# A batched matrix product: loads of four batches at a time, 32 partitions each, with the transposes on VectorE

## The chip, the cores and the metric

The kernel runs on one core of one Trainium2 chip. The metric is the device time of one execution in microseconds; lower is better. The time given for a kernel is the median over several executions. A profile is one execution, recorded by the hardware profiler; its own span is a little shorter than the device time, which also holds what lies around the span.

## The reference

For each of 32 batches, a 256 x 512 matrix is multiplied by a 512 x 384 matrix, all in float32 in memory:

```python
batch, dim_i, dim_j, dim_k = 32, 256, 512, 384
x: (batch, dim_i, dim_j) float32;  y: (batch, dim_j, dim_k) float32
return np.einsum('bij,bjk->bik', x, y).astype(np.float32)
```

TensorE contracts over the partitions of its two operands. y has the contracted index j as its rows already. x has i as its rows, so x has to be transposed on the chip before it can be the stationary operand. Both kernels multiply in float16 and accumulate in float32.

## The kernel before, in words

One batch is one step. In `load(b)` the x of a batch goes to a tile of 128 partitions, partition p holding rows 2p and 2p+1 (L59, runs of 4 KB), and y to a tile whose partition q holds rows 4q to 4q+3 (L60, runs of 6 KB). Both tiles have seven buffers, and loads are issued `AHEAD = 5` batches early. All DMAs, loads and stores, are issued by SyncE (SP) in one queue.

`transpose(b)` takes, for each of the four remainders t of j modulo 4, the columns t, t+4, t+8, ... of x, and transposes two blocks of 128 x 128 on TensorE against an identity matrix (L68), so that partition q of the result holds column 4q+t, in line with y. The result lies in PSUM; VectorE (L70) and ScalarE (L72) copy it to SBUF in turn, rounding to float16 on the way. `round_y(b)` rounds the four slices of y to float16, two on ScalarE (L79) and two on VectorE (L81). `multiply(b)` does 8 matmuls (L92) of 128 contraction rows, 128 output rows and 384 columns into two PSUM tiles. `collect(b)` copies them to SBUF, one on ScalarE (L107), one on VectorE (L109), and `store(b)` writes the batch out (L120, runs of 3 KB).

The order on each engine is the order in which the program is written: every operation is wrapped in `keep`, which holds it in program order. The main loop is a software pipeline: step s issues the loads of batch s+5, collects batch s-2, transposes and rounds batch s, multiplies batch s-1, and stores batch s-2. So the transposes of one batch stand between the multiplications of its neighbours. PSUM is divided into four buffers for transposes and four for results.

Of the kernel before, what the change touches and what calls it, by code (L numbers as in the profile page):

```python
# [1 line left out]

# [5 lines left out]


MM_DT = mybir.dt.float16  # L10
F32 = mybir.dt.float32
P = 128
AHEAD = 5
GROUPS = [1, 1, 1, 1, 1, 1, 1, 1, 1, 1, 1, 1, 1, 1, 1, 1, 1, 1, 1, 1, 1, 1, 1, 1, 1, 1, 1, 1, 1, 1, 1, 1]

@with_exitstack
def kernel(
    ctx: ExitStack,  # L20
    tc: tile.TileContext,
    x: bass.AP,
    y: bass.AP,
    out: bass.AP,
):
    nc = tc.nc

    B, I, J = x.shape
    _, _, K = y.shape

    NI = I // P
    NJ = J // P

    const_pool = ctx.enter_context(tc.tile_pool(name="const", bufs=1))
    x_pool = ctx.enter_context(tc.tile_pool(name="x_pool", bufs=AHEAD + 2))
    y_pool = ctx.enter_context(tc.tile_pool(name="y_pool", bufs=AHEAD + 2))
    yr_pool = ctx.enter_context(tc.tile_pool(name="yr_pool", bufs=4))
    xt_pool = ctx.enter_context(tc.tile_pool(name="xt_pool", bufs=4))
    o_pool = ctx.enter_context(tc.tile_pool(name="o_pool", bufs=8))
    tpsum_pool = ctx.enter_context(tc.tile_pool(name="tpsum", bufs=4, space=bass.MemoryType.PSUM))  # L40
    opsum_pool = ctx.enter_context(tc.tile_pool(name="opsum", bufs=4, space=bass.MemoryType.PSUM))


    keep = tc.keep_in_program_order

    identity = const_pool.tile([P, P], F32)
    make_identity(nc, identity)


    place = [(g, i, n) for g, n in enumerate(GROUPS) for i in range(n)]  # L50
    assert len(place) == B
    x_of, y_of, yr_of, xt_of, ps_of, o_of = {}, {}, {}, {}, {}, {}

    def load(b):


        x_of[b] = x_pool.tile([P, NI, J], F32, name="x_sb")
        y_of[b] = y_pool.tile([P, NJ, K], F32, name="y_sb")
        keep(nc.sync.dma_start(out=x_of[b], in_=x[b].rearrange("(p r) j -> p r j", p=P)))  # L59
        keep(nc.sync.dma_start(out=y_of[b], in_=y[b].rearrange("(q t) k -> q t k", q=P)))  # L60

    def transpose(b):
        x_sb = x_of.pop(b)
        xt_of[b] = xt_pool.tile([P, NJ, NI, P], MM_DT, name="xt_sb")
        for t in range(NJ):
            t_ps = tpsum_pool.tile([P, NI, P], F32, name="t_ps")
            for r in range(NI):
                keep(nc.tensor.transpose(t_ps[:, r], x_sb[:, r, t::NJ], identity))  # L68
            if t % 2 == 0:
                keep(nc.vector.tensor_copy(xt_of[b][:, t], t_ps))  # L70
            else:
                keep(nc.scalar.copy(xt_of[b][:, t], t_ps))  # L72

    def round_y(b):
        y_sb = y_of.pop(b)
        yr_of[b] = yr_pool.tile([P, NJ, K], MM_DT, name="y_r")
        for t in range(NJ):
            if t % 2 == 0:
                keep(nc.scalar.copy(yr_of[b][:, t], y_sb[:, t]))  # L79
            else:  # L80
                keep(nc.vector.tensor_copy(yr_of[b][:, t], y_sb[:, t]))  # L81

    def multiply(b):
        xt_sb, y_r = xt_of.pop(b), yr_of.pop(b)
        ps_of[b] = [
            opsum_pool.tile([P, K], F32, name=f"o_ps_{r}", tag="o_ps")
            for r in range(NI)
        ]
        for t in range(NJ):
            for r in range(NI):  # L90
                keep(
                    nc.tensor.matmul(  # L92
                        ps_of[b][r],
                        xt_sb[:, t, r],
                        y_r[:, t],
                        start=(t == 0),
                        stop=(t == NJ - 1),
                    )
                )

    def collect(b):
        g, i, n = place[b]
        if i == 0:
            o_of[g] = o_pool.tile([P, n, NI, K], F32, name="o_sb", tag=f"o_sb_{min(n, 2)}")
        for r in range(NI):
            if r % 2 == 0:
                keep(nc.scalar.copy(o_of[g][:, i, r], ps_of[b][r]))  # L107
            else:
                keep(nc.vector.tensor_copy(o_of[g][:, i, r], ps_of[b][r]))  # L109
        del ps_of[b]  # L110

    def store(b):
        g, i, n = place[b]
        if i < n - 1:
            return
        o_sb = o_of.pop(g)
        dst = out[b - i : b + 1].rearrange("b (p r) k -> p b (r k)", p=P)
        src = o_sb.rearrange("p b r k -> p b (r k)")
        if n == 1:
            keep(nc.sync.dma_start(out=dst[:, 0], in_=src[:, 0]))  # L120

    for b in range(AHEAD):
        load(b)
    for s in range(B + 2):
        if s + AHEAD < B:
            load(s + AHEAD)
        if s >= 2:
            collect(s - 2)
        if s == B - 1:
            multiply(s - 1)  # L130
        if s < B:
            transpose(s)
            round_y(s)
        if 1 <= s != B - 1 and s <= B:
            multiply(s - 1)
        if s >= 2:
            store(s - 2)


# [1 line left out]
_INS = ['x', 'y']  # L141
_OUTS = [((32, 256, 384), 'float32')]


# [23 lines left out]
```

## Time and profile before

| what | us |
|---|---|
| median of 7 runs | 137.52 (137.13 to 137.62) |
| the profiled execution | 137.17 |
| its span | 135.4 |
| PE busy in the span | 82.3 |
| VectorE (DVE) busy | 64.5 |
| ScalarE (ACT) busy | 66.7 |
| a load of x, issue to landing (median) | 10.2 |
| a load of y, issue to landing (median) | 11.2 |
| a store, issue to landing (median) | 10.9 |

PE is the matmul part of TensorE and PEld its weight loads, which overlap PE. Lines such as L92 are those of the kernel before. Busy time counts work of an engine alone, without the time in which it waits. From memory 41.94 MB are read, and 12.58 MB are written.

### The profile page before, as it was taken

What the parts mean: (1) busy time and instruction counts of PE and PEld (TensorE: products, weight loads), DVE (VectorE), ACT (ScalarE), POOL (GpSimd) and SP (SyncE); (2) the same over time, 40 slices, a digit from 0 to 9 for tenths busy, and PEclk for the clock granted to TensorE, in tenths of its full rate; (3) what the DMA queues carried; (4) which work ended last, traced back from release to release, by engine and by line L of the source; (5) the groups of instructions that cost most, each with busy time, mean ns of one, the idle gap of its engine ahead of it and who ended that gap; (6) DMA issues with size and microseconds to landing.
All of it is one profiled execution on the core that took longest, in us unless ns stands there. A gap on an engine that the chain in (4) does not pass through costs nothing.

```text
span 135.4 us, 1739 instructions
## 1 busy us (share of the span) xinstructions
PE 82.3 (61%) x512; PEld 57.4 (42%) x512; DVE 64.5 (48%) x160; ACT 66.7 (49%) x161; POOL 0.7 (1%) x6
## 2 busy tenths in 40 slices
PE   0589788857255775555775555775555775559610
PEld 0466555525333554333554333554333554435400
DVE  0445766656146644546644546644546644546510
ACT  3357666666056644446644446644446644446610
POOL 2000000000000000000000000000000000000000
PEclk9999999999999999999999999999999999999996
DMA  4999999999999999999999999999999999999992
GB/s 166 418 416 420 418 414 414 375 420 422 409 422 414 426 418 421 416 417 418 428 417 420 416 421 420 426 420 418 414 422 424 413 417 424 418 417 418 412 418 113
DMA packets 13833, 54.64 MB, mean 404 GB/s; under 512 B 1536, under 2 KB 1536, under 8 KB 13824
## 3 DMA queue, kind: packets, MB, share of 16 engines
q1 hardware_dynamic: 13824, 54.53, 98.8%
q8 instruction: 4, 0.07, 0.2%
q14 instruction: 5, 0.04, 0.1%
HBM read 41.94 MB, written 12.58 MB: 403 GB/s over the span
## 4 chain that ended last, share of the span: by engine, by line
DMA 80%; PE 10%; DVE 2%; SPq 2%; issue 1%; ACT 0%; ACTq 0%
DMA x_sb<-in_x_dram 31%; DMA y_sb<-in_y_dram 25%; DMA out_dram<-o_sb 24%; PE o_ps L92 6%; PE t_ps L68 4%; DVE o_sb L109 2%; SPq L59 1%; SPq L60 1%; ACT y_r L79 0%; SPq L120 0%; ACTq L79 0%
## 5 line engine op out<-in xcount | busy, mean ns | idle before, releaser
L68 PE MATMUL t_ps<-identity,x_sb 128*128 128x128 f32 x256 | 39.9, 301 | 45.8 <-DMA x_sb<-in_x_dram 43.2
L68 PEld LDWEIGHTS t_ps<-identity,x_sb 128*128 128x128 f32 x256 | 34.4, 211 | 56.7 <-DVE o_sb L109 42.1
L72 ACT CAST xt_sb<-t_ps 128x256 f16<-128x256 f32 x64 | 23.8, 373 | 54.5 <-issue 43.1
L70 DVE CAST xt_sb<-t_ps 128x256 f16<-128x256 f32 x64 | 27.1, 424 | 48.2 <-PE t_ps L68 46.3
L92 PE MATMUL o_ps<-y_r,xt_sb 128*128 128x384 f16 x256 | 47.4, 329 | 1.2 <-ACT y_r L79 1.2
L79 ACT CAST y_r<-y_sb 128x384 f16<-128x384 f32 x64 | 29.6, 509 | 6.4 <-DMA y_sb<-in_y_dram 6.3
L92 PEld LDWEIGHTS <-xt_sb 128*128 128x128 f16 x256 | 25.7, 100 | 14.8 <-issue 1.9
L81 DVE CAST y_r<-y_sb 128x384 f16<-128x384 f32 x64 | 20.1, 356 | 12.5 <-DMA y_sb<-in_y_dram 12.2
L109 DVE COPY o_sb<-o_ps 128x384 f32<-128x384 f32 x32 | 17.8, 557 | 4.6 <-PE o_ps L92 3.1
L107 ACT COPY o_sb<-o_ps 128x384 f32<-128x384 f32 x32 | 15.1, 472 | 1.2 <-PE o_ps L92 1.2
L72 ACT ACT_TABLE_LOAD x1 | 1.3, 1283 | 0.7 <-PEq L152 0.7
masks.py:199 POOL TENSOR_SCALAR_AFFINE_SELECT identity<-identity 128x128 f32<-128x128 f32 x1 | 0.3, 293 | 0.1
masks.py:197 POOL MEMSET identity<- 128x128 f32 x1 | 0.2, 206 | 0.3 <-POOLq L152 0.3
L152 POOL MEMSET const-bfloat16-1.0<- 128x1 bf16 x1 | 0.1, 102 | 0.0
L152 POOL MEMSET const-uint8-127<- 128x1 uint8 x1 | 0.1, 102 | 0.0
L152 POOL MEMSET const-float32-0.0<- 128x1 f32 x1 | 0.1, 99 | 0.2 <-issue 0.2
L152 POOL MEMSET const-float32-1.0<- 128x1 f32 x1 | 0.1, 99 | 0.0
## 6 DMA issues: line engine op xcount, KB each, us to landing
y_sb<-in_y_dram SPq DMA_DIRECT2D x32, 768.0 KB, 11.2
x_sb<-in_x_dram SPq DMA_DIRECT2D x32, 512.0 KB, 10.2
out_dram<-o_sb SPq DMA_DIRECT2D x32, 384.0 KB, 10.9
```

The lines of the kernel that those rows point to most:

```text
L59: keep(nc.sync.dma_start(out=x_of[b], in_=x[b].rearrange("(p r) j -> p r j", p=P)))
L60: keep(nc.sync.dma_start(out=y_of[b], in_=y[b].rearrange("(q t) k -> q t k", q=P)))
L68: keep(nc.tensor.transpose(t_ps[:, r], x_sb[:, r, t::NJ], identity))
L70: keep(nc.vector.tensor_copy(xt_of[b][:, t], t_ps))
L72: keep(nc.scalar.copy(xt_of[b][:, t], t_ps))
L79: keep(nc.scalar.copy(yr_of[b][:, t], y_sb[:, t]))
L81: keep(nc.vector.tensor_copy(yr_of[b][:, t], y_sb[:, t]))
L92: nc.tensor.matmul(ps_of[b][r], xt_sb[:, t, r], y_r[:, t], start=(t == 0), stop=(t == NJ - 1),)
L107: keep(nc.scalar.copy(o_of[g][:, i, r], ps_of[b][r]))
L109: keep(nc.vector.tensor_copy(o_of[g][:, i, r], ps_of[b][r]))
L152: nc = _bacc.Bacc("TRN2", target_bir_lowering=False, num_devices=1)
```

## The change

Four batches (a "quad") are one step now, and there are eight steps. x of a quad is loaded by one DMA: batch g of the four lies on partitions 32g to 32g+31, each partition holding 8 whole rows of x, one run of 16 KB. y likewise: partition q of a batch's 32 holds rows 16q to 16q+15 of y, one run of 24 KB. In the last quad the load of y is cut in two.

The identity and the TensorE transposes are gone. ScalarE rounds x to float16 and reorders it in the same copy (four copies of 1024 elements per partition, read in steps of 16 float32 elements). VectorE then transposes blocks of 32 x 32 (`nc.vector.transpose`, eight instructions of 512 elements per quad), each group of 32 partitions within itself. After that, partition q of a batch holds the columns 16q+c of x, for c from 0 to 15, in line with y.

Each matmul contracts over 32 partitions only, so a quad has 128 matmuls of 32 x 128 x 384 where four batches had 32 of 128 x 128 x 384. The innermost loop runs over the four batches, so consecutive matmuls use different groups of 32 partitions and different PSUM tiles. The eight PSUM tiles of a quad are all that there are.

y is rounded in eight chunks of 768 elements, five on VectorE and three on ScalarE. In the main loop a quad is transposed, rounded, multiplied and collected to the end before the next is begun; its stores are issued one step later (`LATE = 8`). x and y each have two buffers of a quad: the loads issued in step n are y of quad n+1 and x of quad n+2.

```diff
+Q = 4
+LATE = 8
+LAST = 2
+ROUND = (1, 0, 1, 1, 0, 1, 0, 1)
...
+    S = P // Q
+    R = I // S
+    C = J // S
+    NE = I // P
+    H = R // NE
+    N = B // Q
+    x_pool = ctx.enter_context(tc.tile_pool(name="x_pool", bufs=2))
+    xr_pool = ctx.enter_context(tc.tile_pool(name="xr_pool", bufs=1))
+    xt_pool = ctx.enter_context(tc.tile_pool(name="xt_pool", bufs=2))
+    y_pool = ctx.enter_context(tc.tile_pool(name="y_pool", bufs=2))
+    yr_pool = ctx.enter_context(tc.tile_pool(name="yr_pool", bufs=2))
+    o_pool = ctx.enter_context(tc.tile_pool(name="o_pool", bufs=12))
+    psum_pool = ctx.enter_context(tc.tile_pool(name="psum", bufs=Q * NE, space=bass.MemoryType.PSUM))
...
+    def load_x(n):
+        x_of[n] = x_pool.tile([P, R, J], F32, name="x_sb")
+        keep(nc.sync.dma_start(out=x_of[n],
+                in_=x[n * Q : (n + 1) * Q].rearrange("g (p r) j -> (g p) r j", r=R)))
+    def load_y(n):
+        y_of[n] = y_pool.tile([P, C, K], F32, name="y_sb")
+        src = y[n * Q : (n + 1) * Q].rearrange("g (p c) k -> (g p) c k", c=C)
+        w = C // (LAST if n == N - 1 else 1)
+        for c in range(0, C, w):
+            keep(nc.sync.dma_start(out=y_of[n][:, c : c + w], in_=src[:, c : c + w]))
+    def transpose_x(n):
+        x_sb = x_of.pop(n)
+        xr = xr_pool.tile([P, R, C, S], MM_DT, name="x_r")
+        xt_of[n] = xt_pool.tile([P, C, NE, S, H], MM_DT, name="xt_sb")
+        for h in range(H):
+            rows = slice(h * NE, (h + 1) * NE)
+            keep(nc.scalar.copy(xr[:, rows], x_sb[:, rows].rearrange("q r (j c) -> q r c j", c=C)))
+            for e in range(NE):
+                keep(nc.vector.transpose(xt_of[n][:, :, e, :, h], xr[:, h * NE + e]))
+    def round_y(n):
+        y_sb = y_of.pop(n)
+        y_r = yr_pool.tile([P, C, K], MM_DT, name="y_r")
+        w = C // len(ROUND)
+        for k, dve in enumerate(ROUND):
+            part = slice(k * w, (k + 1) * w)
+            if dve:
+                keep(nc.vector.tensor_copy(y_r[:, part], y_sb[:, part]))
+            else:
+                keep(nc.scalar.copy(y_r[:, part], y_sb[:, part]))
+        return y_r
...
+    def multiply(n, y_r):
+        xt_sb = xt_of.pop(n)
+        ps = [[psum_pool.tile([P, K], F32, name="o_ps") for e in range(NE)] for g in range(Q)]
+        for c in range(C):
+            for e in range(NE):
+                for g in range(Q):
+                    rows = slice(g * S, (g + 1) * S)
+                    keep(nc.tensor.matmul(ps[g][e],
+                            xt_sb[rows, c, e].rearrange("q p h -> q (p h)"),
+                            y_r[rows, c], start=(c == 0), stop=(c == C - 1)))
+        return ps
...
+    def collect(n, ps):
+        for g in range(Q):
+            o_sb = o_of[n * Q + g] = o_pool.tile([P, NE, K], F32, name="o_sb")
+            for e in range(NE):
+                if e % 2 == 0:
+                    keep(nc.scalar.copy(o_sb[:, e], ps[g][e]))
+                else:
+                    keep(nc.vector.tensor_copy(o_sb[:, e], ps[g][e]))
     def store(b):
+        keep(nc.sync.dma_start(out=out[b].rearrange("(m e) k -> m e k", m=P), in_=o_of.pop(b)))
+    load_x(0)
+    load_y(0)
+    load_x(1)
+    for n in range(N + 1):
+        if n + 1 < N:
+            load_y(n + 1)
+        if n + 2 < N:
+            load_x(n + 2)
+        if n < N:
+            transpose_x(n)
+            collect(n, multiply(n, round_y(n)))
+        for b in range(max((n + 1) * Q - LATE, 0), min((n + 2) * Q - LATE, B) if n < N else B):
+            store(b)
```

The lines of the kernel before that these replace are the functions printed above.

## The prediction

> **What bounds the kernel now.** I read the page from the top: the slices (is a resource full throughout?), the chain, the costliest groups (prices), then the trace in windows and as a timeline (what one step looks like).
>
> ```profile
> span 135.4 us, 1739 instructions
> ...
> DMA  4999999999999999999999999999999999999992
> ...
> DMA packets 13833, 54.64 MB, mean 404 GB/s; under 512 B 1536, under 2 KB 1536, under 8 KB 13824
> ...
> DMA 80%; PE 10%; DVE 2%; SPq 2%; issue 1%; ACT 0%; ACTq 0%
> ```
> The 16 DMA engines are full from the first slice to the last, and 80% of the chain that ended last is transfers. Now windows (us, then busy of PE, PEld, DVE, ACT, POOL, then clock, DMA share, GB/s):
>
> ```profile
> 60.00:80.00 20.00, 12.52 (x80) 8.72 (x80) 10.18 (x25) 10.23 (x25) 0.00 (x0) 1.00 1.02 420
> ...
> 131.00:132.00 1.00, 0.00 (x0) 0.00 (x0) 0.00 (x0) 0.00 (x0) 0.00 (x0) 1.00 1.05 421
> 132.00:133.00 1.00, 0.00 (x0) 0.00 (x0) 0.00 (x0) 0.00 (x0) 0.00 (x0) 1.00 0.61 243
> ```
> 420 GB/s in the steady part, still full at 132, while DVE and ACT are half idle. A batch is 1.70 MB (0.52 + 0.79 + 0.39), so 4.06 us at 420, 16.2 us for four; 54.5 MB is 130 us. The rest of the span is start and end. So only fewer bytes, a higher rate or a shorter end would gain; and the engines may slow down until four batches take 16.2 us. Their prices, in groups by line (busy, mean ns, idle and its releaser):
>
> ```profile
> L70 DVE CAST xt_sb<-t_ps 128x256 f16<-128x256 f32 x64 | 27.1, 424 | 48.2 <-PE t_ps L68 46.3
> L92 PE MATMUL o_ps<-y_r,xt_sb 128*128 128x384 f16 x256 | 47.4, 329 | 1.2 <-ACT y_r L79 1.2
> L79 ACT CAST y_r<-y_sb 128x384 f16<-128x384 f32 x64 | 29.6, 509 | 6.4 <-DMA y_sb<-in_y_dram 6.3
> L92 PEld LDWEIGHTS <-xt_sb 128*128 128x128 f16 x256 | 25.7, 100 | 14.8 <-issue 1.9
> L81 DVE CAST y_r<-y_sb 128x384 f16<-128x384 f32 x64 | 20.1, 356 | 12.5 <-DMA y_sb<-in_y_dram 12.2
> L109 DVE COPY o_sb<-o_ps 128x384 f32<-128x384 f32 x32 | 17.8, 557 | 4.6 <-PE o_ps L92 3.1
> L107 ACT COPY o_sb<-o_ps 128x384 f32<-128x384 f32 x32 | 15.1, 472 | 1.2 <-PE o_ps L92 1.2
> ```
> And the timeline, near the start and later (start, length, what):
>
> ```profile
> 9.00 2.19 PE L92 MATMUL o_ps<-y_r,xt_sb 128*128 128x384 f16 x8
> ...
> 9.65 0.15 PEld L92 LDWEIGHTS <-xt_sb 128*128 128x128 f16 x1 [0.17 <-issue]
> 9.97 0.15 PEld L92 LDWEIGHTS <-xt_sb 128*128 128x128 f16 x1 [0.17 <-issue]
> 10.29 0.52 PEld L92 LDWEIGHTS <-xt_sb 128*128 128x128 f16 x3 [0.17 <-issue]
> ...
> 41.96 0.93 ACT L79 CAST y_r<-y_sb 128x384 f16<-128x384 f32 x2 [0.22 <-DMA y_sb<-in_y_dram]
> 41.98 0.63 DVE L81 CAST y_r<-y_sb 128x384 f16<-128x384 f32 x2 [0.44 <-DMA y_sb<-in_y_dram]
> ```
> Two readings. At the start the matmuls of 384 columns follow each other every 0.32 us (9.65, 9.97, 10.29); in the chain of waits, a little later, eight take 1.31 ("14.82 1.31 PE o_ps L92 x8"), so 0.164 each. PE starts at half speed. And a pair back to back takes less than twice its mean: the second of two costs ACT 0.42 (0.93 less 0.51), DVE 0.27. I use such follow-on costs for runs of one kind.
>
> **The Trainium skill.** "TensorE: Matmul & The Clock Gate", Part 1: PE runs at half clock until about 3.4 us of activity, and falls back after an idle window of that order. The trace agrees with the factor (0.32 to 0.164), and its PE gaps of under 2 us don't fall back. Same page, Part 3: matmuls on 32 contraction rows in different row groups run side by side, four of them measured 3.07 times as fast as one after another; no run here shows it. "SBUF — State Buffer", the note on cachelines under "Door 1: The DMA port swizzle": accesses that hop from one 16-byte line to another pay a penalty, two hits on a line absorb it; the trace's strided read (PE's load of x in steps of 16 bytes) shows no doubling at a pair every 0.15 us, but no ACT read of that kind is there. "DMA: Bandwidth & Descriptors", Bandwidth: 425 GB/s for one 16 MB transfer, against 420 here: little to gain.
>
> **The change part by part**, for a quad (four batches).
>
> Bytes: the same. Runs of 4 and 6 KB become 16 and 24 KB, stores stay at 3 KB. Loads (41.9 MB) going from 420 to 425 save 1.2 us in all; bounds 0 and 3.5 (all of the loads at 435). This counts only while DMA sets the pace.
>
> Removed: PE transposes with their eight PSUM copies per batch, and the identity. All lay beside the transfers: worth nothing now.
>
> Added on x: four ACT copies of 1024 elements, each read in steps of 64 bytes, and eight DVE transposes of 512. ACT: the y copy's follow-on of 0.42 for 384 elements, and 640 more at 1.2 GHz (the slope of L79 as the page "VectorE: DVE Perf Modes" prices it), gives 0.95, first one 1.04. If the 64-byte step doubles the element time: 1.80. I take 1.4, the middle, having a page for one end and PE's read for the other. DVE: the microarchitecture page (3.8) says one element per cycle; L70's follow-on is 0.32 for 256, so 0.585 for 512; upper 0.69 if none overlap. Per pair 1.17, below ACT's 1.4, so ACT leads: 4 x 1.4 + two transposes 1.17 + 0.1 handing over = 6.9 us (5.8 with ACT at 0.95, 8.5 at 1.80).
>
> Rounding y: first chunk on DVE (768 elements) 0.56 by L81 plus its slope, then one every 0.46; 0.6 us before the first matmul, the other seven chunks lie beside the matmuls.
>
> Matmuls: 128 per quad in place of 32, 32 contraction rows each, a weight load to each. PE has been idle for the x work (over 7 us), so it begins at half clock: at 3.07-fold, 320/3.07 = 104 ns each for 3.4 us (33 of them), then 164/3.07 = 53 ns for 95: 5.0. Sum 8.5 us. Lower bound 5.2 (perfect fourfold, always warm, 128 x 41 ns); upper 12.8 (weight loads one after another at L92's 100 ns); without overlap 22.6.
>
> Collecting: on each engine four copies follow the last accumulation (c runs outermost, so all eight PSUM banks finish together). ACT 1.6 us, DVE 2.0.
>
> The new wait is the order on the engines: DVE and ACT run x(n), y(n), collect(n), x(n+1). The collects wait for the last matmuls, and behind them in the same queues stand all x(n+1) work, and so PE's next matmuls. Nothing of a quad overlaps the next, except the transfers. Before, transposes of a batch ran beside others' transfers and a batch needed 3.17 us (the chain's transposes at 13.61 and 16.78) of the 4.06. Now the period is ACT's collect 1.6 + x 6.9 + 0.6 + matmuls 8.5 + four handovers 0.2 = 17.8 us, against 16.2 of DMA: the chain becomes the bound.
>
> SP's queue: y(n+1), x(n+2), four stores of quad n-1. A load waits for a buffer that rounding or the ACT copies of two quads earlier freed, a period before its data is needed: hidden. Before, five batches (20 us) were ahead; two quads hold more.
>
> Sum on the profiled run: the first x landed at 4.07 with 0.52 MB; 1.57 MB more at 420 make 7.8; x work to 14.7; y(0), 3.15 MB, lands at 15.3; first matmul 15.9; PE done at 24.4. Seven periods: 149.0. DVE's last collect 151.0. Before, 5.5 us passed from the last store's issue (129.90) to the end with some 1.9 us of other stores ahead of it; here the last four stores need 3.76 us from 149.6 on, so about 1.4 lie ahead: 151.0 + 3.6 + 1.4 = 156.0. Outside the span lie 137.17 - 135.4 = 1.8, and the median is 0.35 above the profiled run: **158 us**. At ACT's ends the same sum gives 150 (period 16.7) and 170 (period 19.4, and x delays the first matmul).
>
> **Rivals.**
> *The chain fits* (0.17): matmuls under about 6 us with ACT at 1.4, or under 6.9 at 0.95, keep up, and DMA stays the bound. For it: PE can overlap weight loads fully (in the trace they hide behind matmuls), eight stores of earlier quads cover the last quad's work. Against it: a cold PE in each quad alone nearly fills 6 us. Time: 137.5 less 1.2 to 3 us, about 135.5.
> *No overlap in PE* (0.10): matmuls of different row groups one after another, or loads that wait for the matmul before. Period 31.9, end near 272. Against it: the skill's measurement.
> *Both upper ends* (0.05): weight loads at 100 ns and ACT doubled: period 23.7, about 205.
> Forecast case: 0.68, own range 142 to 178.
>
> **How the numbers follow.** Leaving out no-overlap, both upper ends and a little of the fast rival gives 134 to 178. What a measurement can tell from no change is about 0.2% (0.27 us). The fast rival splits into 0.14 faster and 0.03 same; all else is slower, 0.83.
>
> **What would show it.** Right: DMA digits with gaps of a tenth or more in every quad; the chain no longer mostly DMA; PE busy in eight blocks of 8 to 9 us with gaps of 9; the ACT x copy at 1.0 to 1.8 us. Wrong: DMA still at nines with a rate near 425, or a PE block of under 6 us (then faster), or blocks of over 20.

## The result, and the profile after

The changed kernel takes 179.54 us (median of 12, 178.53 to 181.22); the kernel before, measured beside it, 137.42 us. The ratio is 1.306, 95% interval 1.304 to 1.309. So the change is 42 us slower: the direction of the forecast, but above its range, which ended at 178. The profiled execution of the changed kernel took 181.22 us, one of its slow runs and 1.7 us above the median, so its span of 179.4 us stands that much too high beside the medians.

The page of the changed kernel, with the rows that answer to those of before: span, PE's granted clock and DMA's share in 40 slices, then the chain by engine.

```profile
span 179.4 us, 2461 instructions
...
PEclk9999999655895559755795559755695559855696
DMA  6999999999996799939997699948999800710027
...
DVE 42%; PE 33%; ACT 13%; DMA 4%; issue 4%; DVEq 0%; ACTq 0%
```

DMA had nines from end to end and 80% of the chain; now it has gaps in every quad, and 4% of the chain. VectorE, PE and ScalarE together hold 88%. PE's clock falls to five again and again; in the kernel before it was at nine until the last slice (at the very start, in both kernels, the row shows nine although the first matmuls took the time of half clock):

```profile
PEclk9999999999999999999999999999999999999996
```

The groups by line (busy us, mean ns of one, idle before and its releaser):

```profile
L110 PE MATMUL o_ps<-y_r,xt_sb 32*128 32x384 f16 x1024 | 60.6, 408 | 112.1 <-DVE y_r L96 112.1
L87 DVE STREAM_TRANSPOSE xt_sb<-x_r 128x512 f16<-128x512 f16 x64 | 74.6, 1334 | 20.0 <-ACT x_r L85 20.0
L85 ACT CAST x_r<-x_sb 128x1024 f16<-128x1024 f32 x32 | 59.5, 1958 | 6.6 <-DMA x_sb<-in_x_dram 6.6
L125 ACT COPY o_sb<-o_ps 128x384 f32<-128x384 f32 x32 | 13.0, 492 | 76.4 <-PE o_ps L110 76.4
L127 DVE COPY o_sb<-o_ps 128x384 f32<-128x384 f32 x32 | 15.6, 550 | 46.3 <-PE o_ps L110 46.3
```

The idle columns show the cycle: PE waits for VectorE's rounding, the collects wait for PE, nothing waits for y (the rounding, L96 and L98, has no idle time before it). One quad of the chain (start, length, what) has the sum itself:

```profile
69.91 0.13 ACT o_sb L125
...
70.27 1.25 ACT o_sb L125 x3
71.52 1.81 ACT x_r L85
...
73.36 5.53 DVE xt_sb L87 x5
...
82.69 0.40 DVE y_r L96
83.09 0.05 issue
83.14 7.36 PE o_ps L110 x118
90.49 0.01 ACT o_sb L125
```

From one end of the matmuls (69.91) to the next (90.49) it is 20.6 us: collecting on ScalarE 1.6 (to 71.52), x 11.2 (to 82.69), the first rounding 0.45, matmuls 7.36. The prediction had 1.6, 6.9, 0.6 and 8.5. Seven periods and the late start of the first (matmuls from 20.35 in place of 15.9) make the difference.

### The profile page after: what moved, and what is told of

Same layout as the page of the kernel before. It is cut to its first block, busy times and chain, and to the rows that moved or that the text cites. A ratio compares the mean times of both kernels' runs of the same rounds, so it can differ in the third digit from the quotient of the medians.

```text
span 179.4 us, 2461 instructions
## 1 busy us (share of the span) xinstructions
PE 60.6 (34%) x1024; PEld 31.4 (18%) x1024; DVE 108.3 (60%) x136; ACT 90.3 (50%) x89; POOL 0.2 (0%) x4
## 4 chain that ended last, share of the span: by engine, by line
DVE 42%; PE 33%; ACT 13%; DMA 4%; issue 4%; DVEq 0%; ACTq 0%
DVE xt_sb L87 40%; PE o_ps L110 33%; ACT x_r L85 8%; ACT o_sb L125 5%; DMA x_sb<-in_x_dram 4%; DVE y_r L96 2%; DVE o_sb L127 1%; DVEq L171 0%; ACTq L125 0%; ACTq L85 0%; DVEq L127 0%
## 5 line engine op out<-in xcount | busy, mean ns | idle before, releaser
L110 PE MATMUL o_ps<-y_r,xt_sb 32*128 32x384 f16 x1024 | 60.6, 408 | 112.1 <-DVE y_r L96 112.1
L87 DVE STREAM_TRANSPOSE xt_sb<-x_r 128x512 f16<-128x512 f16 x64 | 74.6, 1334 | 20.0 <-ACT x_r L85 20.0
L85 ACT CAST x_r<-x_sb 128x1024 f16<-128x1024 f32 x32 | 59.5, 1958 | 6.6 <-DMA x_sb<-in_x_dram 6.6
L110 PEld LDWEIGHTS <-xt_sb 32*128 32x128 f16 x1024 | 31.4, 116 | 140.8 <-DVE y_r L96 94.4
L125 ACT COPY o_sb<-o_ps 128x384 f32<-128x384 f32 x32 | 13.0, 492 | 76.4 <-PE o_ps L110 76.4
L127 DVE COPY o_sb<-o_ps 128x384 f32<-128x384 f32 x32 | 15.6, 550 | 46.3 <-PE o_ps L110 46.3
L96 DVE CAST y_r<-y_sb 128x768 f16<-128x768 f32 x40 | 19.6, 556 | 0.0
L98 ACT CAST y_r<-y_sb 128x768 f16<-128x768 f32 x24 | 18.6, 864 | 0.0
```

The lines of the kernel that those rows point to most:

```text
L85: keep(nc.scalar.copy(xr[:, rows], x_sb[:, rows].rearrange("q r (j c) -> q r c j", c=C)))
L87: keep(nc.vector.transpose(xt_of[n][:, :, e, :, h], xr[:, h * NE + e]))
L96: keep(nc.vector.tensor_copy(y_r[:, part], y_sb[:, part]))
L98: keep(nc.scalar.copy(y_r[:, part], y_sb[:, part]))
L110: nc.tensor.matmul(ps[g][e], xt_sb[rows, c, e].rearrange("q p h -> q (p h)"), y_r[rows, c], start=(c == 0), stop=(c == C - 1),)
L125: keep(nc.scalar.copy(o_sb[:, e], ps[g][e]))
```

## The experiments

All times below are medians (e1 and e8 ran once); each was run beside the kernel before, which took 137.3 to 137.4 us each time.

**Prices alone (e1).** One kernel of VectorE transposes and ScalarE copies, eight or four of each layout.

```diff
+    for r in range(R):
+        keep(nc.vector.transpose(t_whole[:, r], xr[:, r]))
+    for r in range(R):
+        keep(nc.vector.transpose(t_block[:, r % NE, :, r // NE], xr[:, r]))
+    for r in range(R):
+        keep(nc.vector.transpose(t_step[:, :, r % NE, :, r // NE], xr[:, r]))
...
+        keep(nc.scalar.copy(a16[:, rows], x_sb[:, rows].rearrange("q r (j c) -> q r c j", c=C)))
```

> Prices by themselves, with no transfer and no other engine beside them; the product is left out and the output is zeros. Eight VectorE transposes of 512 float16 elements in each of four layouts, eight of float32, and four ScalarE copies of 1024 elements at each of four read steps. Theory W (the 8-byte step of the written elements doubles the transpose): whole and 64-byte runs follow each other every 0.585 us, the 8-byte step every 1.17 us. Rival T (a float16 transpose costs two cycles per element in any layout): all four at 1.17 us. Rival C (contention with ScalarE or the transfers in the changed kernel): all at 0.585 us here. ScalarE: step 1 at 0.95 us, step 16 (64 bytes) at 1.80 us if the read step is the cause, 0.95 us if contention is.

The timeline of e1 (start, length, what; xN is how many follow each other). t_whole is written in one piece, t_block in runs of 64 bytes, t_step as in the changed kernel; t_read is read in steps of 32 bytes; t_f is float32. Then come ScalarE's copies, in order with read steps of 1, 2, 4 and 16 elements (4, 8, 16 and 64 bytes).

```profile
13.18 4.88 DVE L66 STREAM_TRANSPOSE t_whole<-x_r 128x512 f16<-128x512 f16 x8
17.96 4.85 DVE L68 STREAM_TRANSPOSE t_block<-x_r 128x512 f16<-128x512 f16 x8
22.71 9.22 DVE L70 STREAM_TRANSPOSE t_step<-x_r 128x512 f16<-128x512 f16 x8
31.71 7.84 DVE L72 STREAM_TRANSPOSE t_read<-x_r 128x512 f16<-128x512 f16 x8
39.47 4.83 DVE L74 STREAM_TRANSPOSE t_f<-x_sb 128x512 f32<-128x512 f32 x8
...
47.84 3.88 ACT L79 CAST a_step<-x_sb 128x1024 f16<-128x1024 f32 x4
51.63 4.05 ACT L83 CAST a_step<-x_sb 128x1024 f16<-128x1024 f32 x4
55.59 7.64 ACT L87 CAST a_step<-x_sb 128x1024 f16<-128x1024 f32 x4
63.14 7.31 ACT L91 CAST a_step<-x_sb 128x1024 f16<-128x1024 f32 x4
```

From the start of one group to the start of the next, by eight: 0.59 us for a transpose in one piece or in 64-byte runs, 1.13 in 8-byte steps, with no ScalarE beside it. Eight of these take 9.22 us from end to end, and 9.33 in the changed kernel (1.17 each). The expectation says that no transfer runs beside them; in fact the stores of zeros did until about 39 us, but beside the first two layouts as well as the third, so they aren't the difference. So theory W holds, and T and C fall: the write step doubles the transpose, neither the operation nor contention does. The prediction's 0.585 was right for a layout that the kernel doesn't have. ScalarE: 0.95, 0.99, 1.89, then 1.80 for the last (7.31 less one duration of 1.90, by three). Reading in steps of 8 bytes is nearly free; in steps of 16 or 64 bytes the copy takes twice as long. VectorE does the same reordering copy at half the price: e1 makes x_r on VectorE, in four copies of 1024 elements that take 3.83 us, where ScalarE's four take 7.31.

**The order of the quads (e2).**

```diff
+    transpose_x(0)
...
-            transpose_x(n)
-            collect(n, multiply(n, round_y(n)))
+            ps = multiply(n, round_y(n))
+            if n + 1 < N:
+                transpose_x(n + 1)
+            collect(n, ps)
```

> Only the order is changed: x of the next quad is transposed ahead of the collecting of this quad. Theory S (the strict order of the quads sets the 20.7 us period; the sum of VectorE's work alone is 13.7 us, below the 16.2 us of the transfers): the transfers become the bound again, 131 to 138 us. Rival D (the new runs or the two-quad buffers hold the transfers up): stays above 150 us.

143.56 us (ratio 1.038, 1.032 to 1.045), 36 us less than the changed kernel, with every price as it was (transposes 1342 ns on average, copies 1942). Theory S holds for the bulk: moving x(n+1) out from behind collect(n) removes most of the loss. It came out over its 138, and the page of e2 says where:

```profile
DMA  5999999999999999999999999999999999968056
```

DMA is full again for 35 of the 40 slices (to 124 us), and the loss is the end. The last half of y landed at 125, but VectorE had still to transpose x of that quad and to collect the one before it (to 127), and then 128 matmuls, the collects and four stores followed, with too few other stores to cover them.

**The write step in the kernel (e3, e5).** The transposes write runs of 64 bytes; the two kernels differ in how the result goes out.

```diff
-        xt_of[n] = xt_pool.tile([P, C, NE, S, H], MM_DT, name="xt_sb")
+        xt_of[n] = xt_pool.tile([P, NE, C, H, S], MM_DT, name="xt_sb")
...
-                keep(nc.vector.transpose(xt_of[n][:, :, e, :, h], xr[:, h * NE + e]))
+                keep(nc.vector.transpose(xt_of[n][:, e, :, h], xr[:, h * NE + e]))
...
-                            xt_sb[rows, c, e].rearrange("q p h -> q (p h)"),
+                            xt_sb[rows, e, c].rearrange("q h p -> q (h p)"),
```

In e3 `store` has besides:

```diff
...
+        dst = out[b].rearrange("(p h e) k -> h p e k", h=H, e=NE)
+        for h in range(H):
+            keep(nc.sync.dma_start(out=dst[h], in_=o_sb[h * S : (h + 1) * S]))
```

> The transposes write runs of 64 bytes in place of single elements 8 bytes apart; result rows then stand in another order on the partitions, which four stores of 32 partitions a batch put right. Order of the quads as in the changed kernel. Theory W: transposes at 0.585 us, ScalarE's copies lead, x work 8.6 us in place of 11.3, so 8 x 2.7 us less: about 158 us. Rival T: no change, 178 to 181 us.

> As e3, but each batch is stored by one DMA as in the changed kernel, so the rows of the result stand in another order in memory. Theory W: the period of 17.3 us that e3 shows between undisturbed quads, in place of 20.7, in all quads: 8 x 3.4 us less than 179.5, about 152 us. Rival Q (e3's 172 us are what the cheaper transposes are worth, and its 128 stores cost nothing): 170 to 174 us.

e3 took 171.92 us, e5 158.89. In e5 the transposes take 690 ns on average and ScalarE leads the x work: VectorE now waits for it. The timeline of e5 in one quad:

```profile
97.49 7.36 ACT L85 CAST x_r<-x_sb 128x1024 f16<-128x1024 f32 x4
99.46 1.30 DVE L87 STREAM_TRANSPOSE xt_sb<-x_r 128x512 f16<-128x512 f16 x2 [1.35 <-ACT x_r L85]
101.27 1.30 DVE L87 STREAM_TRANSPOSE xt_sb<-x_r 128x512 f16<-128x512 f16 x2 [0.50 <-ACT x_r L85]
```

x takes 8.6 us (97.49 to 106.11, where the rounding begins), as e3's expectation had worked out, and 8 x 2.6 is the 20.6 us that e5 gained. Theory W holds in the kernel too; the 152 us expected for e5 came from one quad of e3 whose matmuls took 6.7 us, where others took up to 8.3. Of the 13 us between e3 and e5, 12 lie at the end. The last quad's matmuls begin at 143.8 us in e3 and at 143.5 in e5, the last collect ends at 153.0 and 152.5; but after it e3 needs another 17.1 us, e5 4.8. The page of e3 shows the rate of its stores in the last slices (4.25 us each):

```profile
GB/s 173 424 457 414 449 439 406 455 393 443 296 182 321 457 370 285 212 348 430 385 256 193 358 420 385 229 216 257 451 393 317 164 319 367 277 144 213 211 210 141
```

Stores of 32 partitions, alone, run at some 211 GB/s, half of the 415 of the stores of 128 partitions in e8 (below), and SP was still issuing the last 48 of them, from 136.8 us on for 31 us. Why they are slow isn't shown. Rival Q falls: the 128 stores do cost time.

**The read step alone (e4), and both prices (e6).**

```diff
-            keep(nc.scalar.copy(xr[:, rows], x_sb[:, rows].rearrange("q r (j c) -> q r c j", c=C)))
+            keep(nc.scalar.copy(xr[:, rows], x_sb[:, rows].rearrange("q r (c j) -> q r c j", c=C)))
```

e6 has this edit and that of e5.

> ScalarE reads x in one piece, without the reordering (the columns of x no longer meet their rows of y, so this is another product of the same size). Theory R (the 64-byte read step doubles ScalarE's copy): copies at 0.95 us in place of 1.81, of which only the first of a quad lies on the path as long as the transposes take 1.17 us each: 8 x 0.9 = 7 us less, about 172 us. Rival: no change, if the copy is slow for another reason.

> Transposes write 64-byte runs and ScalarE reads in one piece (rows of the result in another order, and the columns of x don't meet their rows of y). The order of the quads is that of the changed kernel. This gives both operations the prices that the prediction's lower end assumed (0.585 and 0.95 us). If the prediction's sum is right but for these two terms: x work 5.9 us, period about 16.2 to 16.7, 145 to 151 us. Rival: something else in the sum is wrong, and the time stays above 155 us.

e4 took 178.13 us, only 1.4 less. The copies did fall to 1071 ns, and x to 10.4 us (from 69.66, where the copies start, to 80.05, where the transposes end); but the matmuls rose from 7.4 to 8.26. PE's clock took the gain back: in the timeline of PE's weight loads, the last run without pauses, which is the part at full clock, has 52 loads in e4

```profile
86.22 2.13 PEld L110 LDWEIGHTS <-xt_sb 32*128 32x128 f16 x52 [0.16 <-issue]
```

where the changed kernel has 72:

```profile
87.27 2.95 PEld L110 LDWEIGHTS <-xt_sb 32*128 32x128 f16 x72 [0.16 <-issue]
```

So 20 more matmuls, five groups of four, ran at half clock, 0.16 us each. When the clock comes back doesn't depend on the amount of work alone.

e6 took 140.14 us (ratio 1.022, 1.019 to 1.025), below the 145 expected. Its page:

```profile
DMA  5999999999899999999999999999999999999356
...
DMA 51%; PE 22%; DVE 15%; ACT 7%; issue 1%; DVEq 1%; SPq 0%
```

With both operations at the lower prices even the strict order just fits into the transfers' time. The two prices, then, are worth 39 us together, though 1.4 and 20.6 alone: while one engine leads, the other's gain lies beside it.

**PE's clock (e7, e9).** Zeros are multiplied ahead of each quad's matmuls.

```diff
+        for i in range(WARM):
+            keep(nc.tensor.matmul(ps[0][0], warm_w, warm_v, start=True, stop=True))
```

> Ahead of each quad's matmuls PE runs 64 matmuls of zeros of 128 x 128 x 384, some 10.5 us, while the other engines do the x work. Theory H (PE starts each quad at half speed because it was idle, which costs 14 groups of four at 0.16 us, 2.2 us): matmuls of a quad 5.3 in place of 7.5 us from the second quad on, 15 to 18 us less, about 163 us. Rival L (the first matmuls are slow because they wait for the rounding of y or for weights): no change or slower, 179 us or more.

> As e7 with 76 matmuls of zeros in place of 64, so that the gap before a quad's own matmuls shrinks from 2.25 us to some 0.3 us. Theory H (the granted clock of one half in the 3.4 us after a gap makes the first groups of four take 0.32 us): the clock stays at 1.0 and the 128 matmuls take 5.2 us in place of 7.5, about 163 us, less whatever the zeros delay. Rival M (a mode of 32 rows that follows one of 128 rows, or the weight loads, hold the matmuls at 7 us): as e7, 176 us.

e7 took 176.37 us and looked like a refutation. But its windows (matmuls alone; us, busy of PE, VectorE and ScalarE, clock, DMA share, GB/s) show that the clock fell in spite of the zeros, which had ended 2.24 us ahead of the quad's own matmuls (61.09), and that it fell 0.8 us after these had begun:

```profile
61.00:62.00 1.00, 0.91 (x24) 0.00 (x0) 0.00 (x0) 0.95 1.09 451
62.00:63.00 1.00, 1.00 (x20) 0.00 (x0) 0.00 (x0) 0.50 0.84 328
```

After six of e7's seven gaps of 2.2 us the quad's matmuls took some 7.06 us; after the other one they took 5.38, with the clock at 1.0. With 76 matmuls of zeros in place of 64 the gap is 0.30 us, and e9 took 166.47 us. Windows of e9 (all engines: PE, PEld, DVE, ACT, POOL), one quad's matmuls:

```profile
77.70:82.90 5.20, 5.18 (x128) 3.69 (x127) 1.84 (x4) 0.00 (x0) 0.00 (x0) 1.00 0.96 342
```

against the changed kernel's two parts of such a stretch:

```profile
62.45:66.90 4.45, 4.45 (x56) 2.19 (x60) 1.81 (x4) 0.00 (x0) 0.00 (x0) 0.50 0.95 336
66.90:69.90 3.00, 3.00 (x76) 1.70 (x68) 0.00 (x0) 0.00 (x1) 0.00 (x0) 0.99 1.18 478
```

The clock is at 1.0, and 128 matmuls take 5.2 us: theory H holds, M falls. Idle PE costs the changed kernel 13 us (179.54 to 166.47); 3.5 us of the gain expected didn't come. Some 1 us of it is the first quad, where the zeros had ended 3.9 us ahead and the matmuls took 7.06 us; the rest the runs don't explain.

**The transfers alone (e8).**

```diff
+    for b in range(B // 2):
...
+        keep(nc.sync.dma_start(out=x_small, in_=x[b].rearrange("(p r) j -> p r j", p=P)))
+        keep(nc.sync.dma_start(out=y_small, in_=y[b].rearrange("(q t) k -> q t k", q=P)))
+    for n in range(N // 2, N):
...
+        keep(nc.sync.dma_start(out=x_large, in_=x[n * Q : (n + 1) * Q].rearrange("g (p r) j -> (g p) r j", r=R)))
+        keep(nc.sync.dma_start(out=y_large, in_=y[n * Q : (n + 1) * Q].rearrange("g (p c) k -> (g p) c k", c=C)))
```

> Transfers alone: half of the loads with the runs of the kernel before (4 and 6 KB), then half with those of the changed kernel (16 and 24 KB), then the stores, of zeros; no product. Theory N (long runs bring next to nothing): 415 to 425 GB/s in both halves. Rival G (long runs are faster, as slices of 450 GB/s in the changed kernel suggest): 440 or more in the second half.

The windows of e8 (busy of VectorE and GpSimd, clock, DMA share, GB/s); the short runs end near 53 us (21 MB at 415), the loads near 102:

```profile
20.00:40.00 20.00, 0.00 (x0) 0.00 (x0) 1.00 1.02 414
...
60.00:80.00 20.00, 0.00 (x0) 0.00 (x0) 1.00 1.00 428
80.00:100.00 20.00, 0.00 (x0) 0.00 (x0) 1.00 1.02 437
...
110.00:130.00 20.00, 0.00 (x0) 0.00 (x0) 1.00 1.03 415
```

Long runs bring 3 to 5% on loads alone, between theory and rival; the stores stay at 415. All of it took 135.15 us: the kernel before stands 2 us above bare transfers, loads first and then stores, and there was little for any change of the engines to win.

**A version of the whole product (e10, e11).** Pairs of float16 values are transposed as 4-byte elements, and the order is that of a pipeline; e11 has `LATE = 12` and 16 result buffers besides.

```diff
+            keep(nc.scalar.copy(xr_of[n][:, :, h // 2, :, :, h % 2], x_sb[:, rows].rearrange("q r (j c) -> q r c j", c=C)))
...
+        for h in range(0, H, 2):
             for e in range(NE):
+                keep(nc.vector.transpose(
+                        xt_of[n][:, :, e, :, h : h + 2].bitcast(F32)[:, :, :, 0],
+                        xr[:, e, h // 2].bitcast(F32)[:, :, :, 0]))
...
+            ps = multiply(n, round_y(n))
+            if n + 1 < N:
+                copy_x(n + 1)
+            collect(n, ps)
+            if n + 1 < N:
+                transpose_x(n + 1)
```

> The whole product. Two float16 values of one column are transposed as one 4-byte element, so a quad has four VectorE transposes in place of eight; ScalarE copies x of the next quad ahead of its collecting, and VectorE transposes it behind its own. Theory S: ScalarE 11.3 us and VectorE some 9 us a quad lie below the 16.2 us of the transfers, which become the bound; the last y lands near 122 us and 13 us of work follow: 134 to 139 us. Rival: a 4-byte element written in steps of 8 bytes, or a ScalarE copy that writes in steps of 4 bytes, costs over twice as much, and the time stays above 142 us.

> As e10, with the stores held back one more quad (16 result buffers), so the last y lands 3.7 us earlier and the last quad's work has more stores to hide it. Theory E (the work after the last y sets the end in e10): 2 to 3.7 us less than e10, 131 to 136 us. Rival: no change, if the transfers' total sets the end.

e10 took 139.73 us (ratio 1.017, 1.015 to 1.020), e11 138.84 (1.010, 1.007 to 1.012), both a little above their expectations. A pair as one element is written in the same 8-byte steps and yet not slower than in one piece; the group of e10:

```profile
L95 DVE STREAM_TRANSPOSE xt_sb<-x_r 128x512 f32<-128x512 f32 x32 | 20.8, 690 | 23.6 <-ACT x_r L86 23.6
```

So it is the 2-byte element in such steps that costs double, not the step alone. e11's page and windows (all engines, clock, DMA share, GB/s at the end):

```profile
DMA  5999999999999999999999999999999999999971
```

```profile
100.00:110.00 10.00, 5.57 (x72) 2.73 (x76) 3.74 (x7) 4.07 (x9) 0.00 (x0) 0.50 1.00 406
110.00:120.00 10.00, 3.60 (x76) 1.75 (x68) 5.85 (x11) 9.49 (x9) 0.00 (x0) 0.84 1.00 393
```

The transfers are full up to the last two slices, and this kernel is still 1% slower than the one before: where loads in long runs are mixed with stores, the rate is 393 to 425 GB/s, no better than the 409 to 421 of before. Theory E gained 0.9 of its 2 us; after that DMA, full almost to the end, seems to be the limit. Why the mixed stream loses what the long loads gain in e8 stays open. Of the versions run, none beats the kernel before.

## Why the prediction was wrong in size and right in kind

- *Which resource bounds, before and after.* Right. The chain passes from DMA (80%) to the engines, by the order on VectorE and ScalarE that the prediction named; e2, which changes only that order, shows it.
- *VectorE's transposes: the step that failed.* "DVE: ... one element per cycle; L70's follow-on is 0.32 for 256, so 0.585 for 512; upper 0.69 if none overlap." It was 1.17, outside its own bounds, because both bounds priced the operation and neither its output pattern, single 2-byte elements 8 bytes apart (e1 shows that the pattern doubles it, e5 that this is worth 20.6 us in the kernel). The diff shows that pattern in the transpose's destination. With it fell the sentence that a pair stays "below ACT's 1.4, so ACT leads": a pair takes 2.3, and VectorE led. This is the step that carried the time out of the range: with ScalarE doubled and VectorE as priced, the prediction's own sum gives 170.
- *ScalarE's copies.* 1.4 was taken between 0.95 and 1.80; it was 1.81 (e1, and the chain). The bound was right, the middle wasn't. The Trainium skill's note on cachelines ("SBUF — State Buffer", under "Door 1: The DMA port swizzle") says that two hits on a 16-byte line absorb the latency and that crossing to a new line each time costs; e1 agrees, with 0.99 us in steps of 8 bytes (two elements a line) and 1.89 in steps of 16 (one). The note gives no size for the penalty; here it is twofold. Its example, that one can stride over 4 fp32 for free, doesn't hold here for a step of four. It doesn't account for VectorE's write, where two elements fall on each line and the price doubles all the same (1.13); why that is stays open. PE's strided load of before was no guide to ScalarE.
- *Matmuls.* 8.5 was taken, 7.4 measured. The overlap is complete; the 3.07-fold of the Trainium skill ("TensorE: Matmul & The Clock Gate", Part 3) was too low for these matmuls: four matmuls in 0.32 us at half clock and 0.16 at full clock, where single ones took 0.32 and 0.164 before. The half clock was seen rightly (it lasted 4.45 us of a quad, not 3.4), and costs 13 us in all (e9). That gaps of under 2 us don't bring it back holds in the trace of before, but the length of a gap doesn't decide by itself: the same trace has one of 3.19 us (before 36.22) after which eight transposes took 1.21 us, the price at full clock (1.95 at the start), and in e7 the clock fell after 2.2.
- *Collecting, rounding, end.* 1.6, 0.45 and 6.7 us (172.67 to 179.4), against 1.6, 0.6 and 7.0.
- *The sum.* x was 4.3 us a quad too low, PE 1.1 too high, rounding and handovers 0.3: 2.8 net over seven periods is 19.6, and 4.0 more in the first quad make the 23.4 us between 156.0 and 179.4. About 1.8 us lie outside the span in both. Of these 23.4 us some 1.7 belong to the profiled execution; between the medians, 158 and 179.5, it is 21.5.
- *The range.* It stopped at the doubled ScalarE copy. A quad with both doubled prices and the measured matmuls has 20.6 us; the prediction's "both upper ends" doubled ScalarE and PE's loads, not VectorE.
- *Rivals.* "The chain fits" is what e6 does at 140 us, once both prices are the low ones. "No overlap in PE" is excluded: its 22.6 us for a quad's matmuls were 7.4.

## What to carry to other kernels

Price an instruction with its access pattern, output too: here an operand that hops, a 2-byte one written every 8 bytes on VectorE or a 4-byte one read every 16 on ScalarE, cost as much as twice the elements, and a bound on a price that leaves the pattern out is no bound. Where all transfers are full and the engines half idle, ask first how far bare transfers lie below; here 2 us. When the next step's work stands in a queue behind the end of this step, its whole price lands on the path, so that a change of order (e2, 36 us) can be worth more than either price alone (1.4 and 20.6 us).

## What the runs showed of the hardware that was not expected

- A VectorE transpose of 512 elements follows another after 0.59 us with 2- or 4-byte elements, written in one piece or in 64-byte runs; after 1.13 us with 2-byte elements written 8 bytes apart (e1), and after 0.97 when read 32 bytes apart; a 4-byte element written 8 bytes apart costs no more than in one piece (e10: mean 690 ns against 684 in e1).
- ScalarE's copy of 1024 float32 elements: 0.95 us read in one piece, 0.99 in steps of 8 bytes, 1.8 to 1.9 in steps of 16 or 64. VectorE's takes 0.96 us in steps of 64 bytes (3.83 for four, e1).
- PE's granted clock fell to 0.5, for 3.4 us in the quad shown, after six of seven gaps of 2.2 us (e7), but not after one of 3.19 us in the kernel before, and not after gaps of 0.30 us (e9); multiplications of zeros kept it at 1.0. What decides between these gaps isn't shown. A quad can so lose in PE what it gained on x (e4).
- Stores of 32 partitions ran at 211 GB/s (e3, end), those of 128 partitions at 415 (e8).
- Four matmuls of 32 contraction rows in four row groups take the time of one of 128 rows: 0.16 us at full clock (128 in 5.2 us, e9), against 0.164 before.
